# A two-part transformer at 256 positions in split float32: feed-forward products 512 columns wide, and the modulation rows summed on the vector engine

## The chip, the cores and the metric

The kernel runs on one core of one Trainium2 chip, as one program. The metric is device time in microseconds (us); lower is better. A core has a matrix engine (PE, with its weight loads shown as PEld), a vector engine (DVE), an activation engine (ACT), a general engine (POOL), a queue for transfers (SP) and 16 DMA engines. PE reads the on-chip memory SBUF and writes PSUM, which has eight banks of 2 KB for each of 128 partitions; a bank holds 512 float32 columns. Each engine works through its own instructions in order.

## The reference, cut to what matters

The input `x` has 256 positions of 1024 features. A first block does mixed attention, cross attention and a feed-forward. Two further layers follow, whose norms are shifted, scaled and gated by rows computed from a vector `c` ("modulation"). In each of them a gated feed-forward stands before and after a mixer.

```python
# first block
u = rms_norm(x, g_mlp[l]) @ w_up[l]                     # 1024 -> 4096
x = x + jnp.square(jax.nn.relu(u)) @ w_down[l]          # 4096 -> 1024
...
# second block, two layers
mod = c_act @ ada_w[l] + ada_b[l]                       # 1024 -> 9 * 1024
sh1, sc1, g1, sh2, sc2, g2, sh3, sc3, g3 = jnp.split(mod, N_ADA, axis=-1)
h = modulate(x, norm_g[l, 0], sh1, sc1)
x = x + 0.5 * g1[:, None] * swiglu(h, ff_w13[l, 0], ff_w2[l, 0])   # a, b = h @ w13; (silu(a) * b) @ w2
...                                                     # layer 0: convolution and attention; layer 1: sparse attention
h = modulate(x, norm_g[l, 2], sh3, sc3)
x = x + 0.5 * g3[:, None] * swiglu(h, ff_w13[l, 1], ff_w2[l, 1])
```

The inner width of `swiglu` is 2816, which is 22 blocks of 128. `c_act` is the SiLU of `c`.

## The kernel before

Everything is held transposed: features on the 128 partitions, the 256 positions (`S`) as columns. A weight matrix is cut into tiles of 128 x 128. To keep float32 accuracy with PE's faster 32-bit form (`fp32r`), each weight and each activation is split in two: a rounded `hi` and the rest `lo = value - hi`. A product is three matmuls, `hi*hi + hi*lo + lo*hi`, all added up in PSUM (`mm3`, line 358): weights `wh`, `wl` are PE's stationary operand, activations `xh`, `xl` its moving one, 256 columns each time. Every matmul loads its own weights.

Weights stream in units of 1 MB (`raw`, [128 x 2048], four buffers, issued on SP in `issue`, line 386). `pump` (line 402) splits half a unit at a time: ACT writes `whi` (line 329), DVE writes `wlo` (line 415), three half units ahead of use. A half unit feeds 8 weight tiles and is called a *step* here. The program is a list of steps in an order written out in Python, and every engine's order follows from it.

`pairs` (line 462) makes two blocks of 128 outputs at a time: 2 x 8 weight tiles, two steps, both results side by side in one PSUM bank. It serves `w_up` (16 pairs), `w13` (22 pairs, four times) and smaller products. The first 2 or 3 pairs of a `w13` (`head`) have a form of their own, with two more columns for the shift. `singles` (line 516) makes one block of 128 outputs at a time; without `early` it serves `w_down` (8 blocks of 32 tiles) and `w2` (8 blocks of 22 tiles, four times).

After a pair, `evac_up` (line 1353) or `evac` in `ff` (line 1403) takes the result out of PSUM (ReLU and square, or SiLU and product, on DVE and ACT), and the result is split into `gh` (ACT) and `gl` (DVE, line 353), deferred to the next step. After a single, `evac` in `residual` (line 1268) adds it to `x` (DVE, line 1271 or 1273), and `norm_part` starts the next norm from it.

The modulation rows are the second stream. `ada_steps` (line 714) needs 9 x 8 slices of [128 x 1024] for each of two layers, two slices to a unit of 1 MB that goes through the same four `raw` buffers. Each slice is times one number per partition and added up in `adacc`: for the first slice of a sum ACT writes `adacc`; for the other seven ACT scales the slice in place and POOL adds it (line 737), in halves of 512 columns. `with_ada` (line 783) spreads these pieces behind the steps from the first attention to the middle of the third `w2`. `rows` then lets PE add up `adacc` over the partitions, two steps after the last piece.

`self.g` gives [128 x 256] buffers from a ring of 64 (`GP`). The lines on which the counting of matmuls and of modulation pieces rests (361 and 736 to 737):

```python
prod = [(wh, xh), (wh, xl), (wl, xh)]
...
self.act(src, src, scale=scale)
nc.gpsimd.tensor_tensor(half, half, src, OP.add)
```

## Time and profile before

| | us |
|---|---|
| median of 3 runs | 1494.89 (1494.23 to 1496.46) |
| the profiled execution | 1491.65 |
| its span, first to last instruction | 1489.9 |
| PE busy in the span | 1437.3 |
| DVE busy | 1059.5 |
| ACT busy | 918.9 |
| POOL busy | 633.6 |

A line of a profile names line, engine, operation, the tiles written and read, shapes, count, busy time, the mean of one in ns, and what ended the engine's idle time before it. PE's matmuls overlap, so the time that one costs is the distance from its start to the next one's start, not its row's duration.

### The profile page before, as it was taken

Reading aid. Unit: us, or ns where it says so; the run is one execution under the profiler, and the core shown is the slowest. Engines: PE = TensorE matmul, PEld = TensorE weight load, DVE = VectorE, ACT = ScalarE, POOL = GpSimd, SP = SyncE. Lnnn points to the kernel's source line nnn. Section 1 sums busy time; section 2 is a strip of 40 time slices with the busy share of each in tenths; the row PEclk is TensorE's granted clock in tenths of the full one; section 3 lists DMA queues with packets and bytes.
Section 4 is the critical chain, followed back from the end, with each engine's and each line's share of the span. In section 5 each row is a group of like instructions: output and inputs, shape, how many; then the busy total and the mean of one; then the engine's idle time right before and its main releaser. Section 6 shows DMA issues by size and latency. Waiting matters only on the chain.

```text
span 1489.9 us, 28338 instructions
## 1 busy us (share of the span) xinstructions
PE 1437.3 (96%) x11478; PEld 1374.9 (92%) x11478; DVE 1059.5 (71%) x1643; ACT 918.9 (62%) x1666; POOL 633.6 (43%) x466
## 2 busy tenths in 40 slices
PE   8998999999999999998899999999999999999997
PEld 8886989999989989998799999999999887999997
DVE  7877767776658777689887776677765788765553
ACT  6546767777657567664667666676654665644442
POOL 3002433545874566753356658546453200500021
PEclk9999999999999999999999999999999999999998
DMA  8344646777665777754447877568773620355451
GB/s 319 116 142 170 218 151 227 244 270 273 260 246 199 278 267 272 257 186 170 169 171 272 295 262 296 206 238 300 259 278 132 219 80 25 118 198 196 173 182 45
DMA packets 46067, 312.00 MB, mean 209 GB/s; under 512 B 5232, under 2 KB 7024, under 8 KB 9072
## 3 DMA queue, kind: packets, MB, share of 16 engines
q1 hardware_dynamic: 45936, 310.19, 57.8%
q8 instruction: 90, 1.47, 0.4%
q14 instruction: 41, 0.34, 0.1%
HBM read 309.12 MB, written 1.05 MB: 208 GB/s over the span
## 4 chain that ended last, share of the span: by engine, by line
PE 64%; DVE 16%; ACT 8%; DMA 7%; issue 2%; POOL 1%; SPq 0%; POOLq 0%; ACTq 0%; DVEq 0%
PE mm L356 57%; DVE wlo L415 6%; DMA raw<-w 4%; ACT whi L329 2%; ACT raw L329 2%; PE sc L356 2%; PE o L356 1%; DVE p L849 1%; POOL adacc L737 1%; PE mmt L356 1%; DVE hlo L664 1%; DMA raw<-w_up 1%; DMA raw<-w_down 1%; DVE gl L353 1%; ACT p L329 1%
## 5 line engine op out<-in xcount | busy, mean ns | idle before, releaser
L415 DVE TENSOR_TENSOR wlo<-raw,whi 128x1024 fp32r<-128x1024 f32 (+2 forms) x438 | 627.2, 1438 | 52.2 <-ACT whi L329 51.7
L737 POOL TENSOR_TENSOR adacc<-adacc,raw 128x512 f32<-128x512 f32 x252 | 430.8, 1734 | 415.8 <-ACT raw L329 331.4
L356 PE MATMUL mm<-hlo,whi 128*128 128x256 f32 x1960 | 556.6, 284 | 6.0 <-DVE hlo L664 4.1
L356 PE MATMUL mm<-hhi,whi 128*128 128x256 f32 (+1 forms) x1960 | 558.0, 285 | 1.5 <-ACT whi L329 1.5
L356 PE MATMUL mm<-hhi,wlo 128*128 128x256 f32 (+1 forms) x1960 | 553.3, 282 | 5.2 <-DVE wlo L415 5.2
L329 ACT ACTIVATE whi<-raw 128x1024 fp32r<-128x1024 f32 (+2 forms) x438 | 453.2, 1044 | 110.6 <-DMA raw<-w 72.5
L356 PEld LDWEIGHTS mm<-hlo,whi 128*128 128x128 f32 x1960 | 369.9, 189 | 9.6 <-DVE hlo L664 5.6
L356 PEld LDWEIGHTS mm<-hhi,wlo 128*128 128x128 f32 x1960 | 371.2, 189 | 7.3 <-DVE wlo L415 7.0
L356 PEld LDWEIGHTS mm<-hhi,whi 128*128 128x128 f32 x1960 | 370.2, 189 | 5.4 <-DVE wlo L415 1.7
L356 PE MATMUL mm<-gh,whi 128*128 128x256 f32 x960 | 272.6, 284 | 0.0
L356 PE MATMUL mm<-gh,wlo 128*128 128x256 f32 x960 | 271.6, 283 | 0.0
L356 PE MATMUL mm<-gl,whi 128*128 128x256 f32 x960 | 271.6, 283 | 0.0
L356 PEld LDWEIGHTS mm<-gh,whi 128*128 128x128 f32 x960 | 184.2, 192 | 4.3 <-issue 3.4
L356 PEld LDWEIGHTS mm<-gl,whi 128*128 128x128 f32 x960 | 184.2, 192 | 0.0
L356 PEld LDWEIGHTS mm<-gh,wlo 128*128 128x128 f32 x960 | 184.2, 192 | 0.0
L329 ACT ACTIVATE raw<-raw,sc 128x512 f32<-128x512 f32 x252 | 167.0, 712 | 0.6 <-DMA raw<-ada 0.5
L1410 DVE TENSOR_TENSOR ft<-mm,ft 128x256 f32<-128x256 f32 x79 | 33.4, 423 | 110.0 <-ACT ft L329 109.8
L353 DVE TENSOR_TENSOR gl<-ft,gh 128x256 fp32r<-128x256 f32 x120 | 74.0, 628 | 46.2 <-ACT gh L329 46.0
L580 POOL TENSOR_SCALAR xg<-x,M 128x256 f32<-128x256 f32 x40 | 55.9, 1398 | 97.4 <-DVE x L1273 91.2
L329 ACT ACTIVATE p<-sc,nm 128x128 f32<-128x128 f32 (+1 forms) x120 | 49.8, 420 | 66.5 <-DVE r L840 18.7
L329 ACT ACTIVATE ft<-mm 128x256 f32<-128x256 f32 x79 | 29.9, 379 | 96.3 <-PE mm L356 96.1
L596 POOL TENSOR_TENSOR acc<-acc,sq 128x256 f32<-128x256 f32 x60 | 60.8, 1016 | 43.5 <-ACT sq L329 37.0
(298 smaller groups left out, 1878.6 us busy)
## 6 DMA issues: line engine op xcount, KB each, us to landing
raw<-w SPq DMA_DIRECT2D x132, 1024.0 KB, 4.9
raw<-ada SPq DMA_DIRECT2D x72, 1024.0 KB, 6.4
raw<-w_up SPq DMA_DIRECT2D x16, 1024.0 KB, 5.0
raw<-w_down SPq DMA_DIRECT2D x16, 1024.0 KB, 5.2
raw<-hy_in SPq DMA_DIRECT2D x8, 1024.0 KB, 5.2
raw<-w_in SPq DMA_DIRECT2D x6, 1024.0 KB, 7.8
raw<-nsa_in SPq DMA_DIRECT2D x6, 1024.0 KB, 5.0
raw<-w_ck SPq DMA_DIRECT2D x4, 1024.0 KB, 4.9
```

What stands on the lines that cost most here:

```text
L329: return self.nc.scalar.activation(out, in_, func, **k)
L353: self.nc.vector.tensor_tensor(lo, src, hi.bitcast(F), OP.subtract)
L356: self.nc.tensor.matmul(out, lhsT, rhs, start=start, stop=stop, skip_group_check=True)
L415: self.behind = lambda hi=hi[:, :b - a], lo=lo[:, :b - a], src=src: self.nc.vector.tensor_tensor(lo, src, hi.bitcast(F), OP.subtract)
L580: nc.gpsimd.tensor_scalar(st["xg", c], xc, gain(c), None, op0=OP.mult)
L596: nc.gpsimd.tensor_tensor(acc, st["acc" + key], sq, OP.add)
L664: nc.vector.scalar_tensor_tensor(*last, op0=OP.add, op1=OP.subtract)
L737: nc.gpsimd.tensor_tensor(half, half, src, OP.add)
L849: nc.vector.tensor_scalar(p[n], p[n], r[:, n:n + 1], None, op0=OP.mult)
L1410: nc.vector.tensor_mul(s, ps[:, 1, :], s)
```

## The change

Four things change.

1. Activations are held as one buffer with `lo` and `hi` side by side (`h`: [`lo` | `hi` | two shift columns] for each block; `gg` and others through `two`: [`hi` | `lo`]). For `w_up`, for the `w13` pairs behind the heads and for `w_down` and `w2`, a weight tile takes two matmuls and not three: `wh` against both halves, 512 columns, into a whole PSUM bank, and `wl` against the `hi` half, 256 columns, added to one half of that bank (`mm2`). The other products keep three.
2. The two halves of the bank are joined after the product: in `pairs` by `summed` (ACT copies one half, DVE adds the other), with the rest of `evac` deferred by one step and the split by two; in `residual` by a second addition to `x`. A wide pair uses two banks, one from tag `mm` and one from tag `T`; the banks of `ada` move from `T` to `O`.
3. A modulation slice is one instruction of 1024 columns: ACT for the first of a sum, DVE's scalar_tensor_tensor (times the number, plus `adacc`) for the other seven. ACT's scaling and POOL's additions are gone.
4. `self.g` gives halves of [128 x 2 x 256] buffers from a ring of 32.

```diff
+    def summed(self, pss):
+        ts = [self.t("ft") for _ in pss]
+        for t, ps in zip(ts, pss):
+            self.act(t, ps[:, 0, :])
+        for t, ps in zip(ts, pss):
+            self.nc.vector.tensor_add(t, ps[:, 1, :], t)
+        return ts
...
+    def mm2(self, out, w, x, start, stop):
+        (wh, wl), (xh, _, both) = w, x[:3]
+        self.mm(out.rearrange("p a b -> p (a b)"), wh, both, start=start, stop=False)
+        self.mm(out[:, self.hi_at(x), :], wl, xh, start=False, stop=stop)
...
     def flush(self):
-        for f in self.deferred:
+        now, self.deferred = self.deferred, []
+        for f in now:
             f()
-        self.deferred.clear()
...
-                        if r == 0:
+                        if r == 0 and wide:
+                            state["ps"] = [self.ps("mm", [P, 2, S], "mm"), self.ps("mm", [P, 2, S], "T")]
+                        elif r == 0:
                             state["ps"] = self.ps("mm", [P, 2, S], tags[pr % 2])
-                        self.mm3(state["ps"][:, m, :], w, (xh, xl), start=r == 0, stop=k == kc - 1)
+                        if wide:
+                            self.mm2(state["ps"][m], w, x(k), start=k == 0, stop=k == kc - 1)
+                        else:
+                            self.mm3w(state["ps"][:, m, :], w, (xh, xl), start=r == 0, stop=k == kc - 1)
...
             def fn(raw):
-                if k == 0 and b == 0:
+                if k == 0:
                     st["acc", s] = self.w("adacc", [P, D], bufs=2)
...
                 if k == 0:
-                    self.act(half, src, scale=scale)
+                    self.act(acc, src, scale=scale)
...
                 else:
-                    self.act(src, src, scale=scale)
-                    nc.gpsimd.tensor_tensor(half, half, src, OP.add)
+                    nc.vector.scalar_tensor_tensor(acc, src, scale, acc, op0=OP.mult, op1=OP.add)
...
-                if gate is None:
-                    nc.vector.tensor_add(xc, ps, xc)
-                else:
-                    nc.vector.scalar_tensor_tensor(xc, ps, gate(m), xc, op0=OP.mult, op1=OP.add)
+                for part in (ps,) if len(ps.shape) == 2 else (ps[:, 0, :], ps[:, 1, :]):
+                    if gate is None:
+                        nc.vector.tensor_add(xc, part, xc)
+                    else:
+                        nc.vector.scalar_tensor_tensor(xc, part, gate(m), xc, op0=OP.mult, op1=OP.add)
...
-                nc.vector.scalar_tensor_tensor(t, ps[:, m, :], 0.0, stu["rbs"], op0=OP.max, op1=OP.mult)
-                self.act(t, t, AF.Square)
...
+            for m, t in enumerate(self.summed(ps)):
+                g = gg[2 * pr + m] = self.two("gg")
+                def up(g=g, t=t):
+                    nc.vector.scalar_tensor_tensor(t, t, 0.0, stu["rbs"], op0=OP.max, op1=OP.mult)
+                    self.act(t, t, AF.Square)
+                    self.deferred.append(lambda: self.split(g[0], g[1], t))
+                self.deferred.append(up)
...
-                self.act(s, ps[:, 0, :], AF.Silu)
-                nc.vector.tensor_mul(s, ps[:, 1, :], s)
...
+            s, t = self.summed(ps)
+            def up():
+                self.act(s, s, AF.Silu)
+                nc.vector.tensor_mul(s, t, s)
+                self.deferred.append(lambda: self.split(g[0], g[1], s))
+            self.deferred.append(up)
```

PE at the border of two pairs in the second `w13`. `mm` is the PSUM bank, `hhi`, `hlo` and `h` are the activations, `whi` and `wlo` the weights. Before, the last tile of one pair and the first of the next:

```order
L356 MATMUL mm_10694<-hhi_9006,whi_10611 128x256
L356 MATMUL mm_10694<-hlo_9007,whi_10611 128x256
L356 MATMUL mm_10694<-hhi_9006,wlo_10612 128x256
L356 MATMUL mm_10764<-hhi_9006,whi_10647 128x256
L356 MATMUL mm_10764<-hlo_9007,whi_10647 128x256
L356 MATMUL mm_10764<-hhi_9006,wlo_10648 128x256
```

After, the last tile of one pair and the first two of the next:

```order
L385 MATMUL mm_8896<-h_7818,whi_8828 128x512
L385 MATMUL mm_8896<-h_7818,wlo_8829 128x256
L385 MATMUL mm_8951<-h_7818,whi_8855 128x512
L385 MATMUL mm_8951<-h_7818,wlo_8856 128x256
L385 MATMUL mm_8952<-h_7818,whi_8855 128x512
L385 MATMUL mm_8952<-h_7818,wlo_8856 128x256
```

A tile has two rows and not three, and the two results of a pair stand in two banks.

DVE in the same `w13`, a little over one pair. `ft` is the pair's result on its way, `gl` and `gg` the split result, `adacc` the modulation sum. Before:

```order
L1410 TENSOR_TENSOR ft_10675<-mm_10619,ft_10675 128x256
L415 TENSOR_TENSOR wlo_10648<-raw_10464,whi_10647 128x1024
L353 TENSOR_TENSOR gl_10679<-ft_10675,gh_10678 128x256
L415 TENSOR_TENSOR wlo_10687<-raw_10464,whi_10686 128x1024
L1410 TENSOR_TENSOR ft_10747<-mm_10694,ft_10747 128x256
L415 TENSOR_TENSOR wlo_10720<-raw_10615,whi_10719 128x1024
```

After:

```order
L377 TENSOR_TENSOR ft_8936<-mm_8895,ft_8936 128x256
L377 TENSOR_TENSOR ft_8937<-mm_8896,ft_8937 128x256
L785 SCALAR_TENSOR_TENSOR adacc_8739<-raw_8777,sc_683,adacc_8739 128x1024
L456 TENSOR_TENSOR wlo_8914<-raw_8832,whi_8913 128x1024
L1466 TENSOR_TENSOR ft_8936<-ft_8937,ft_8936 128x256
L785 SCALAR_TENSOR_TENSOR adacc_8739<-raw_8777,sc_683,adacc_8739 128x1024
L456 TENSOR_TENSOR wlo_8944<-raw_8832,whi_8943 128x1024
L382 TENSOR_TENSOR gg_8935<-ft_8936,gg_8935 128x256
```

Between two weight splits there now stand two joins, or a modulation slice, that were not on DVE; this pair has two slices, others have one or none.

ACT in the same place. `raw` scaled in place is the modulation slice. Before:

```order
L329 ACTIVATE whi_10719<-raw_10615 128x1024
L329 ACTIVATE ft_10747<-mm_10694 128x256
L329 ACTIVATE raw_10539<-raw_10539,sc_707 128x512 x2
L329 ACTIVATE whi_10756<-raw_10615 128x1024
L329 ACTIVATE gh_10750<-ft_10747 128x256
```

After:

```order
L349 ACTIVATE gg_8877<-ft_8878 128x256
L349 ACTIVATE ft_8936<-mm_8895 128x256
L349 ACTIVATE ft_8937<-mm_8896 128x256
L349 ACTIVATE whi_8943<-raw_8832 128x1024
L349 ACTIVATE ft_8936<-ft_8936 128x256
```

Two copies out of PSUM stand where the SiLU stood, the SiLU (`ft<-ft`) comes one weight split later, and the two scalings are gone.

## Rows read from the trace of the kernel before

**Rows 1.** The page: busy time of each engine, share of the span, instructions.

```profile
PE 1437.3 (96%) x11478; PEld 1374.9 (92%) x11478; DVE 1059.5 (71%) x1643; ACT 918.9 (62%) x1666; POOL 633.6 (43%) x466
```

**Rows 2.** The chain in order of time: start, length, what (us).

```profile
773.22 83.28 PE mm L356 x695
...
1304.67 167.41 PE mm L356 x1397
```

**Rows 3.** Stretches: length, then busy PE, PEld, DVE, ACT, POOL; clock, DMA share, GB/s.

```profile
265.00:343.00 78.00, 75.52 (x618) 73.14 (x617) 58.37 (x76) 59.40 (x106) 42.86 (x28) 1.00 0.74 261
...
643.00:756.00 113.00, 100.65 (x774) 92.50 (x773) 97.56 (x179) 67.88 (x142) 48.19 (x45) 0.98 0.48 171
...
776.00:887.00 111.00, 111.00 (x931) 110.03 (x930) 80.45 (x85) 78.23 (x124) 65.39 (x36) 1.00 0.76 273
...
1306.00:1416.00 110.00, 110.00 (x924) 110.00 (x923) 61.21 (x84) 50.84 (x79) 0.00 (x0) 1.00 0.55 192
```

**Rows 4.** The page's costliest groups.

```profile
L737 POOL TENSOR_TENSOR adacc<-adacc,raw 128x512 f32<-128x512 f32 x252 | 430.8, 1734 | 415.8 <-ACT raw L329 331.4
...
L329 ACT ACTIVATE whi<-raw 128x1024 fp32r<-128x1024 f32 (+2 forms) x438 | 453.2, 1044 | 110.6 <-DMA raw<-w 72.5
...
L356 PE MATMUL mm<-gh,whi 128*128 128x256 f32 x960 | 272.6, 284 | 0.0
...
L329 ACT ACTIVATE raw<-raw,sc 128x512 f32<-128x512 f32 x252 | 167.0, 712 | 0.6 <-DMA raw<-ada 0.5
...
L329 ACT ACTIVATE ft<-mm 128x256 f32<-128x256 f32 x79 | 29.9, 379 | 96.3 <-PE mm L356 96.1
```

**Rows 5.** PE in order of time, in the cross-attention values: start, duration, what (us).

```profile
133.88 0.39 PE L356 MATMUL mm<-wlo,hmh 128*128 128x512 f32 x1
...
135.04 0.39 PE L356 MATMUL mm<-whi,hmh 128*128 128x512 f32 x1
135.27 0.39 PE L356 MATMUL mm<-wlo,hmh 128*128 128x512 f32 x1
...
136.17 0.39 PE L356 MATMUL mm<-whi,hml 128*128 128x512 f32 x1
```

**Rows 6.** What PE waited for: total us, times, longest.

```profile
PE mm L356 <- DVE wlo L415: 5.2, 8, 1.9
...
PE ada L356 <- POOL adacc L737: 3.8, 4, 1.2
```

**Rows 7.** DVE in order of time in the second `w13` (us).

```profile
802.10 0.51 DVE L353 TENSOR_TENSOR gl<-ft,gh 128x256 fp32r<-128x256 f32 x1 [0.92 <-ACT gh L329]
802.53 2.31 DVE L415 TENSOR_TENSOR wlo<-raw,whi 128x1024 fp32r<-128x1024 f32 x1
805.36 0.42 DVE L1410 TENSOR_TENSOR ft<-mm,ft 128x256 f32<-128x256 f32 x1 [0.51 <-ACT ft L329]
...
811.11 0.42 DVE L1410 TENSOR_TENSOR ft<-mm,ft 128x256 f32<-128x256 f32 x1 [1.47 <-ACT ft L329]
811.45 1.22 DVE L415 TENSOR_TENSOR wlo<-raw,whi 128x1024 fp32r<-128x1024 f32 x1
```

**Rows 8.** DVE's groups in 776 to 887 us, the second `w13`.

```profile
L353 DVE TENSOR_TENSOR gl<-ft,gh 128x256 fp32r<-128x256 f32 x20 | 13.6, 678 | 10.1 <-ACT gh L329 10.1
L1410 DVE TENSOR_TENSOR ft<-mm,ft 128x256 f32<-128x256 f32 x19 | 8.0, 424 | 19.1 <-ACT ft L329 19.1
```

**Rows 9.** DVE's groups in 265 to 343 us, `w_up`.

```profile
L1356 DVE SCALAR_TENSOR_TENSOR ft<-mm,rbs 128x256 f32<-128x256 f32 x24 | 8.9, 412 | 1.0 <-PE mm L356 1.0
```

**Rows 10.** DVE's groups in 887 to 954 us, the second `w2`.

```profile
L1273 DVE SCALAR_TENSOR_TENSOR x<-mm,M,x 128x256 f32<-128x256 f32 x7 | 3.3, 477 | 1.9 <-PE mm L356 1.9
```

**Rows 11.** POOL's modulation additions by stretch: length, busy POOL (count), clock, DMA share, GB/s.

```profile
265.00:343.00 78.00, 42.86 (x28) 1.00 0.74 261
643.00:756.00 113.00, 20.92 (x16) 0.98 0.48 171
776.00:887.00 111.00, 65.39 (x36) 1.00 0.76 273
```

More of the change, by code (lines that the diff above doesn't have):

```diff
@@ L303, in __init__, with two @@
         self.flip, self.now = 0, None
+        self.half = {}
         self.deferred, self.behind = [], None
     def g(self, name, dt=F, shape=None):
-        return self.gp.tile(shape or [P, S], dt, name=name, tag="g")
+        key = (name if name in PAIRED else "", dt)
+        t = self.half.pop(key, None)
+        n = 1
+        if t is None:
+            n = 0
+            t = self.half[key] = self.gp.tile([P, 2, S], dt, name=name, tag="g")
+        ap = t[:, n, :]
+        if shape:
+            names = " ".join(f"d{i}" for i in range(len(shape) - 1))
+            ap = ap.rearrange(f"p ({names}) -> p {names}", **{f"d{i}": x for i, x in enumerate(shape[1:])})
+        return ap
+    def two(self, name):
+        if name == "gg":
+            self.half.clear()
+        t = self.gp.tile([P, 2, S], R, name=name, tag="g")
+        return t[:, 0, :], t[:, 1, :], t.rearrange("p a b -> p (a b)")
     def w(self, name, shape, dt=F, tag=None, bufs=2):
@@ L495, in fn @@
                     w = (hi[:, o:o + P], lo[:, o:o + P])
[L496 to L497 removed]
+                    xh, xl = x(k)[:2]
                     if pr < head:
@@ L703, in dst, with h_part @@
             if c == 0:
[L704 to L708 removed]
+                self.h = self.work.tile([P, KD, 2 * S + 2], R, name="h", tag="h", bufs=1)
+            return self.h_part(c)
+        return dst
+    def h_part(self, c):
+        return self.h[:, c, S:2 * S], self.h[:, c, :S], self.h[:, c, :2 * S], None
     def h_src(self):
[L711 removed]
+        return self.h_part
     def ada_steps(self, l):
@@ L776, in ada_steps @@
             for q in range(4):
-                steps.append([piece(s, q, n) for n in range(4)])
+                steps.append([piece(s, q, n) for n in range(2)])
             if s % 2 or s == 8:
@@ L899, in split_out @@
     def split_out(self, ps, name, scale=None):
-        hi, lo = self.g(name + "h", R), self.g(name + "l", R)
+        pair = self.two(name)
+        hi, lo = pair[:2]
         if scale is None:
@@ L905, in split_out @@
             self.nc.vector.scalar_tensor_tensor(lo, ps, scale, hi.bitcast(F), op0=OP.mult, op1=OP.subtract)
-        return hi, lo
+        return pair
     def zeroed(self, name, keep):
@@ L965, in late_loads @@
         nc.sync.dma_start(self.posi[1], self.dram["pos"][:, 1, :])
-        self.mem = [self.g(f"mem{c}") for c in range(KD)]
+        self.mem = [self.g("mem") for c in range(KD)]
         for c in range(KD):
@@ L1067, in mdst @@
         def mdst(c):
-            hm[c] = (self.g(f"hmh{c}", R), self.g(f"hml{c}", R))
+            hm[c] = self.two("hm")
             return hm[c]
@@ L1353, in evac_up @@
         def evac_up(pr, ps):
-            for m in range(2):
-                t = self.t("ft")
-                nc.vector.scalar_tensor_tensor(t, ps[:, m, :], 0.0, stu["rbs"], op0=OP.max, op1=OP.mult)
-                self.act(t, t, AF.Square)
-                gh, gl = self.g("gh", R), self.g("gl", R)
-                self.deferred.append(lambda gh=gh, gl=gl, t=t: self.split(gh, gl, t))
-                gg[2 * pr + m] = (gh, gl)
-        gsrc = (lambda k: gg[k][0], lambda k: gg[k][1])
+            for m, t in enumerate(self.summed(ps)):
[5 more added lines that the diff above has]
+                self.deferred.append(up)
+        gsrc = lambda k: gg[k]
         self.gg, self.gsrc = gg, gsrc
-        mlp = self.pairs("w_up", h, KD, evac_up, npairs=16, st=stu)
+        mlp = self.pairs("w_up", h, KD, evac_up, npairs=16, st=stu, wide=True)
         M = self.M[0]
@@ L1460, in evac_z @@
                         nc.vector.tensor_mul(a, src, a)
-                        hi, lo = self.g("yh", R), self.g("yl", R)
-                        self.split(hi, lo, a)
-                        y[c] = (hi, lo)
+                        y[c] = self.two("y")
+                        self.split(y[c][0], y[c][1], a)
         scale = 96 ** -0.5
```

99 lines of the change are left out of this document (48 added, 51 removed).

## The prediction

> **What bounds the kernel now.** I read the page's busy times first: PE 96% of the span, DVE 71%, ACT 62%, POOL 43% [rows 1]. A busy PE can still be waiting between matmuls, so the second view is the chain in order of time: in the second `w13` it is PE alone for 83.28 us and 695 matmuls, and in the last feed-forward for 167.41 us and 1397 [rows 2]. That is 0.1198 us from start to start both times: PE runs without a hole. The third view, stretches, says where this holds. In the second `w13` PE is busy for all of 111.0 us beside a DVE of 80.5, ACT of 78.2 and POOL of 65.4; in the last `w13`, which has no modulation work, for all of 110.0 [rows 3]. In `w_up` 75.5 of 78 are left, and in the mixer of layer 0 100.7 of 113, with DVE at 97.6 [rows 3]. The granted clock is 1.00 in the feed-forwards, the upper level of 2.4 GHz. So the feed-forwards, two thirds of the span, are bound by the time of a matmul; there an instruction taken from PE counts in full if weights and PSUM come free as fast. In the mixers the small waits between engines decide, and PE gains nothing there.
>
> **Matmuls, the main term.** The wide tiles are: `w_up` 16 pairs x 16 = 256, `w13` (4 x 22 - 9 head pairs) x 16 = 1264, `w_down` 8 x 32 = 256, `w2` 4 x 8 x 22 = 704; together 2480. (The last two are the 960 `gh` matmuls of each kind [rows 4].) A tile now costs 3 x 0.1198 = 0.3595 us. After, it is one matmul of 512 columns and one of 256. The cross-attention values have 512-column matmuls of the same kind, each with its own weights: 133.88 to 136.17 us is ten distances, 0.229 each [rows 5]. No row has 512 followed by 256 into half the bank, so the sum 0.229 + 0.1198 = 0.3488 is an estimate; it saves 0.0107 us a tile, **26.5 us** in all. Bounds: the five distances from 133.88 to 135.04 give 0.232, the four from 135.27 to 136.17 give 0.225 [rows 5]; with these a tile saves 0.0077 or 0.0147 us, 19.1 or 36.5 us in all. I take the mean of the ten, as `wh` and `wl` follow each other here as there.
>
> The Trainium skill (TensorE: Matmul & The Clock Gate, Back-to-back issue gap) gives columns / 2.4 GHz plus 2.5 ns per matmul at the full clock, 109 ns for 256 columns and 216 for 512; by that a merge would save 2.5 ns a tile, 6.2 us in all. The trace differs, with 119.8 and 229, so by its rows the part of a matmul that does not grow with its columns is about 10.7 ns. A rival below is built on this doubt.
>
> **Modulation, off POOL and ACT.** POOL loses all 252 additions, 430.8 us, and ACT 252 scalings of 0.71 us [rows 4]. DVE gains 126 instructions of 1024 columns. Before has none; a weight split of that size takes 1.22 us when POOL is quiet [rows 7], and a number per partition adds 0.05 (0.477 against 0.424 on 256 columns [rows 8, 10]), so 1.27; four 256-column ones, 1.91, are the upper bound, 1.22 the lower. In a row of DVE instructions the next starts 0.08 us before the row of the last ends (811.11 plus 0.42 against 811.45 [rows 7]), so each costs the queue 0.08 less: 1.19. In return DVE is no longer slowed: the split takes 2.31 beside POOL and 1.22 without [rows 7].
>
> **Does DVE keep up?** Per pair of a `w13`: two splits of 1.14, two joins, one product and one `lo` of 0.34, together 3.64 us. The second `w13` has 36 half additions in 111 us [rows 11], so 18 slices over some 19.3 pairs, 0.93 x 1.19 = 1.10. Sum 4.74 against 16 x 0.3488 = 5.58 of PE. With 1.91 it is 5.3, still below. So the added DVE work is hidden under PE; without that cover 18 slices and 39 joins would be 35 us here alone. In `w_up` a pair has two ReLUs (0.33 each, from PSUM [rows 9]) and two `lo`: 4.30, plus 14 slices over 13 pairs [rows 11], 1.28, makes 5.58 against 5.58: a tie. With 1.91 it is 6.27, 9 us over the 13 pairs. I take 2 us for a tie that is not always hit, 0 to 9 as bounds. Behind a waiting slice on DVE stand the next weight split and the joins; the split due next is needed two steps, 5.6 us, after the pair's end and would be done 3.6 after it (a copy of 0.38, two joins, a slice, the split), so some 2 us of a delay are hidden.
>
> ACT in the second `w13` loses 36 x 0.71 = 25.6 of 78.2 us and gains about 20 copies of 0.38 [rows 3, 4, 11]. It is nowhere near the bound. The joins also stand between a pair and its split, but the value is first read in `w2` after 21 tiles, 7 us later: nothing. The ring of 32 double buffers holds as much as the 64; I cost it at nothing, since what is paired is made and read together.
>
> **Waits.** PE waited 3.8 us in four places for POOL's last addition before `rows` [rows 6]. DVE has two whole steps for it, about 5.6 us: **-3.8**. The 5.2 us for `wlo` [rows 6] I leave as they are; POOL's absence shortens them, DVE's new work lengthens them. The second addition to `x` is behind the last matmul of the whole kernel: 0.477 less the overlap, **+0.4**. At the four inner ends of a feed-forward the same 0.4 stands before a norm that PE reaches only after a further step: 0, at most 2. In the mixer of layer 0 16 half additions, 8 slices, fall on a DVE that is busy 97.6 of 113 [rows 3, 11]: if all lie on the path +9.5; the 20.9 us of POOL that now leave DVE alone give back up to half, -10, and ACT loses 16 x 0.71. I take 0, and 5 either way for all mixers. SP's order of transfers is unchanged; a modulation unit's buffer is given back by DVE and not by POOL.
>
> **Sum** on the profiled execution: 1491.65 - 26.5 + 2 - 3.8 + 0.4 = 1463.8. It was 3.2 us below the median of the runs, so I forecast 1467 us.
>
> **Rival 1: the weight stream does not go faster.** Four `raw` buffers carry both streams. DMA is busy 0.76 in the second `w13` against 0.55 in the last [rows 3], and ACT's `whi` waited 72.5 us for weights in all [rows 4]. If the ring is at its limit wherever both streams run, only the other tiles gain: three pairs of `w_up`, the last `w13` and `w2`, 48 + 320 + 176 = 544 x 0.0107 = 5.8 us, and 1494.9 - 5.8 + 0.4 = 1489.5. Against it: PE shows no hole there [rows 2], ACT waits with three half units in hand, and the wish is for 3% more on 0.76. Chance 0.10.
>
> **Rival 2: a merge saves nothing.** If the 0.229 of 512 columns owes something to that stretch and a matmul's time goes with its columns alone, 512 take 2 x 0.1198, and only the waits are won: 1494.9 - 3.8 + 0.4 = 1491.5. Against it: the ten distances, with a spread of 3%, lie below 0.2396 [rows 5]. Chance 0.05. The Trainium skill's 2.5 ns a matmul, named above, lies between this and the forecast, at 1494.9 - 6.2 - 3.4 = 1485; the same ten distances speak against it, and it has no more than a part of the 0.05.
>
> **Rival 3, slower: DVE waits in its own order.** In the second `w13` DVE stood idle 10.1 us before 20 `gl`, waiting for ACT, and 19.1 before 19 products [rows 8], 1.5 us per pair. Some of that is only DVE being early: the 1.47 and 0.51 before the product wait for PE's pair by way of ACT, but the 0.92 before `gl` is ACT's order [rows 7]. The joins and the deferred product add links DVE-ACT-DVE. If 1.5 us a pair stay, a `w13` pair with slices takes 6.24 and a `w_up` pair 7.08, against 5.75 and 6.0 (78 us / 13) before: 59 x 0.49 + 13 x 1.08 = +43 us, less 14.2 on the other 1328 tiles and 3.8: 1494.9 + 25 = 1520. It decides from 1.15 us a pair on. Against it: a weight split stands between each pair of links, 1.14 us in which ACT can answer, and ACT's scalings, which held `gh` back, are gone. Chance 0.07.
>
> **How the numbers follow.** Forecast 0.72, rival 1 0.10, rival 2 0.05, rival 3 0.07, and 0.06 for more than forecast (mixers freed of POOL, the fast bound of a tile), below 1455. The range goes from 1455 (the fast bound of a tile: 1494.9 - 36.5 - 3.8 + 0.4) up to rival 1 at 1489.5, and so takes in the slow tile together with 9 us in `w_up` (1482); it leaves out 0.18. Faster by over 0.2% (3 us, about what a measurement of this kernel can tell from no change): 0.72 + 0.10 + 0.06 + part of rival 2 = 0.90; within: 0.03; slower: 0.07.
>
> **What would show it.** PE's chain in the second `w13` at 0.349 us for two matmuls, its 20 wide pairs ending some 3.4 us earlier; POOL's `adacc` rows gone and `wlo` at 1.22 everywhere in `w13`; DVE at 85% there and near full in `w_up`; no wait of PE for `adacc`. Wrong, if 512 followed by 256 takes 0.36 (rival 2), if PE waits for `wlo` behind a DMA (rival 1) or for `wlo` and joins with DVE idle before ACT (rival 3).

## The result and the profile after

The changed kernel takes **1458.78 us** (median of 4 runs, 1455.91 to 1460.99) against 1495.2 of the kernel before beside it (4 runs, 1494.23 to 1496.46): ratio **0.9755, 95% interval 0.9735 to 0.9775**. The forecast was 1467 in a range of 1455 to 1489.5. The profiled execution took 1455.91 us, with a span of 1453.8; that of before had 1489.9.

First the page's busy times (busy us, share of the span, instructions), which answer [rows 1], and pieces of the chain in order of time (start, length, what), which answer [rows 2]:

```profile
PE 1410.9 (97%) x8998; PEld 1243.0 (85%) x8998; DVE 1156.2 (80%) x1999; ACT 821.8 (57%) x1586; POOL 212.0 (15%) x214
```

```profile
584.11 39.38 PE mm L385 x227
...
751.93 81.71 PE mm L385 x464
...
1271.98 163.22 PE mm L385 x932
```

The chain through these feed-forwards is still PE alone, with two matmuls to a tile and not three: 81.71 us for 464 is 0.352 us a tile in the second `w13`; 39.38 for 227 is 0.347 in a `w2`. Before, three made 0.3595. The same stretches as [rows 3], in the same columns (`w_up`, mixer of layer 0, second and last `w13`):

```profile
262.00:337.00 75.00, 73.58 (x416) 63.10 (x418) 70.19 (x113) 47.96 (x98) 0.00 (x0) 1.00 0.73 272
...
623.00:735.00 112.00, 102.04 (x780) 94.27 (x779) 95.11 (x188) 59.53 (x127) 27.33 (x30) 0.97 0.46 166
755.00:863.00 108.00, 108.00 (x620) 93.76 (x619) 93.68 (x139) 67.40 (x122) 0.00 (x0) 1.00 0.76 282
1274.00:1381.00 107.00, 107.00 (x612) 93.69 (x611) 73.43 (x122) 63.30 (x117) 0.00 (x0) 1.00 0.55 194
```

POOL's column is empty in the feed-forward stretches, DVE's has risen from 80.45 of 111 to 93.68 of 108 in the second `w13` and from 58.37 of 78 to 70.19 of 75 in `w_up`, and PE is busy in all or nearly all of each feed-forward stretch. Next the page's groups (instructions, busy us, mean ns, idle before and who ended it), to be read beside [rows 4]:

```profile
L456 DVE TENSOR_TENSOR wlo<-raw,whi 128x1024 fp32r<-128x1024 f32 (+2 forms) x438 | 539.2, 1236 | 11.3 <-ACT whi L349 10.6
...
L349 ACT ACTIVATE whi<-raw 128x1024 fp32r<-128x1024 f32 (+2 forms) x438 | 452.0, 1046 | 119.3 <-DMA raw<-w 80.8
L785 DVE SCALAR_TENSOR_TENSOR adacc<-raw,sc,adacc 128x1024 f32<-128x1024 f32 x126 | 164.0, 1301 | 0.2 <-ACT adacc L349 0.2
L377 DVE TENSOR_TENSOR ft<-mm,ft 128x256 f32<-128x256 f32 x190 | 72.1, 419 | 48.9 <-ACT ft L349 48.8
```

The 126 slices are on DVE at 1.30 us; the 252 rows of POOL are gone, and `wlo` has a mean of 1.236 us. The joins are the 190 rows of the helper's line 377. What PE's matmuls waited for (us in all, times, longest), against [rows 6]:

```profile
PE sc L385 <- ACT p L349: 6.1, 6, 2.6
PE mm L385 <- DVE h L714: 4.4, 7, 1.1
PE mm L385 <- DVE q L1557: 3.5, 1, 3.5
PE mm L385 <- DVE wlo L456: 3.5, 6, 1.0
```

No row of `adacc` is left. A stage ledger shows where the 36 us lie. It goes from each stage's first matmul to the next one's, in us; the middle column is the first experiment below, where the modulation alone is moved.

| stage | before | modulation moved | changed |
|---|---|---|---|
| start to `w_up` | 243.1 | 241.3 | 241.2 |
| `w_up` | 100.2 | 95.7 | 96.5 |
| `w_down` | 97.5 | 94.3 | 92.8 |
| `w13`, `w2` | 136.6, 65.1 | 131.4, 65.1 | 129.7, 62.8 |
| mixer of layer 0 | 113.6 | 111.8 | 111.8 |
| `w13`, `w2` | 130.5, 67.7 | 130.5, 65.0 | 128.4, 62.8 |
| `w13`, `w2` | 130.6, 65.5 | 130.6, 65.1 | 128.4, 63.6 |
| mixer of layer 1 | 137.2 | 136.4 | 136.8 |
| `w13`, `w2` and end | 128.9, 73.4 | 128.9, 73.6 | 126.8, 72.2 |

### The profile page after: what moved, and what is told of

The parts are those of the page before. It is cut to its first block, busy times and chain, and to the rows that moved or that the text cites. A ratio compares the mean times of both kernels' runs of the same rounds, so it can differ in the third digit from the quotient of the medians.

```text
span 1453.8 us, 23211 instructions
## 1 busy us (share of the span) xinstructions
PE 1410.9 (97%) x8998; PEld 1243.0 (85%) x8998; DVE 1156.2 (80%) x1999; ACT 821.8 (57%) x1586; POOL 212.0 (15%) x214
## 3 DMA queue, kind: packets, MB, share of 16 engines
q8 instruction: 70, 1.15, 0.3%
## 4 chain that ended last, share of the span: by engine, by line
PE 76%; DVE 16%; ACT 4%; DMA 2%; issue 2%; POOL 0%; SPq 0%; POOLq 0%; ACTq 0%; DVEq 0%
PE mm L385 68%; DVE wlo L456 4%; DVE adacc L785 2%; PE sc L385 2%; PE o L385 2%; PE mmt L385 1%; DVE h L714 1%; ACT p L349 1%; DVE gg L382 1%; DMA raw<-w_in 1%; ACT whi L349 1%; PE ada L385 1%; PE pT L904 1%; DVE p L897 1%; PE ssum L385 1%
## 5 line engine op out<-in xcount | busy, mean ns | idle before, releaser
L385 PE MATMUL mm<-h,whi 128*128 128x512 f32 (+2 forms) x2400 | 710.1, 358 | 6.3 <-DVE h L714 4.4
L385 PE MATMUL mm<-h,wlo 128*128 128x256 f32 (+1 forms) x1960 | 553.6, 282 | 3.5 <-DVE wlo L456 3.5
L456 DVE TENSOR_TENSOR wlo<-raw,whi 128x1024 fp32r<-128x1024 f32 (+2 forms) x438 | 539.2, 1236 | 11.3 <-ACT whi L349 10.6
L349 ACT ACTIVATE whi<-raw 128x1024 fp32r<-128x1024 f32 (+2 forms) x438 | 452.0, 1046 | 119.3 <-DMA raw<-w 80.8
L385 PEld LDWEIGHTS mm<-h,whi 128*128 128x128 f32 x2400 | 425.9, 190 | 80.9 <-DVE h L714 8.2
L385 PEld LDWEIGHTS mm<-h,wlo 128*128 128x128 f32 x1960 | 371.3, 189 | 6.3 <-DVE wlo L456 5.9
L385 PE MATMUL mm<-gg,whi 128*128 128x512 f32 x960 | 337.1, 397 | 0.0
L385 PE MATMUL mm<-gg,wlo 128*128 128x256 f32 x960 | 267.5, 279 | 0.0
L385 PEld LDWEIGHTS mm<-gg,whi 128*128 128x128 f32 x960 | 180.2, 188 | 46.9 <-issue 4.2
L385 PEld LDWEIGHTS mm<-gg,wlo 128*128 128x128 f32 x960 | 180.7, 188 | 0.1
L785 DVE SCALAR_TENSOR_TENSOR adacc<-raw,sc,adacc 128x1024 f32<-128x1024 f32 x126 | 164.0, 1301 | 0.2 <-ACT adacc L349 0.2
L349 ACT ACTIVATE ft<-mm 128x256 f32<-128x256 f32 x190 | 65.5, 377 | 73.1 <-PE mm L385 72.9
```

Of the source, the lines that this page charges most:

```text
L349: return self.nc.scalar.activation(out, in_, func, **k)
L385: self.nc.tensor.matmul(out, lhsT, rhs, start=start, stop=stop, skip_group_check=True)
L456: self.behind = lambda hi=hi[:, :b - a], lo=lo[:, :b - a], src=src: self.nc.vector.tensor_tensor(lo, src, hi.bitcast(F), OP.subtract)
L785: nc.vector.scalar_tensor_tensor(acc, src, scale, acc, op0=OP.mult, op1=OP.add)
```

## Experiments

Two theories divide the 36 us that were won. **A**: some 22 come from the merged matmuls, between the prediction's slow bound of 19.1 and its 26.5, and some 14 from moving the modulation off POOL and ACT. **B**: the move wins the 4 us of the prediction, and the merge some 32. The first runs left a third question: why the move is worth so much. Every ratio below is to the kernel before, run beside that experiment; its own median lay between 1491.9 and 1495.9 us.

**e1_ada_dve: the modulation alone.** The kernel before, with this:

```diff
-ADA_LAGS = (0, 0, 1, 1, 3, 4)
+ADA_LAGS = (0, 1, 3, 4)
...
-                    self.act(src, src, scale=scale)
-                    nc.gpsimd.tensor_tensor(half, half, src, OP.add)
+                    nc.vector.scalar_tensor_tensor(acc, src, scale, acc, op0=OP.mult, op1=OP.add)
```

> The kernel before, with the modulation slices as 126 scalar_tensor_tensors of 1024 columns on DVE and nothing else of the change: three matmuls per tile, buffers and joins as before. Theory A (the change won some 22 us from merged matmuls and some 14 us from taking the modulation off POOL and ACT): 1495 - 14 = 1481 us, with the time won at the places where PE waited for POOL's last addition and for wlo. Theory B (nearly all of the 36 us is from the matmuls, the modulation is worth the 3.8 us that PE waited for POOL): 1491 us.

Measured: 1472.74 us, ratio 0.9866 (0.9843 to 0.9889), span 1469.7: 20 us, more than either theory gave. The view the prediction left out is what PE's weight loads waited for, here of the kernel before (us in all, times, longest):

```profile
PEld ada L356 <- POOL adacc L737: 9.7, 9, 2.1
PEld mm L356 <- DVE wlo L415: 8.6, 11, 2.1
```

A matmul's weights are loaded ahead of it, and where the stationary operand is the late one (`adacc` is that of `rows`) the wait stands in the load's row. From the matmul before `rows` to the one after it, four of the ten groups took 3.01 to 4.36 us in the kernel before; in this run all take 1.19 to 1.21. The sum over the ten is 10.9 us, not the 3.8 of the matmuls' own rows [rows 6]. The ledger's first `w_up`, `w_down`, `w13` and the second `w2` hold them. The rest, some 9 us, lies in the same stages, in the start and in the mixer; PE's waits for `wlo` fall from 5.2 us to 1.8 in the matmuls' view.

Where the rest may come from, the chain shows. Here is a piece of it in `w_up` of the kernel before (start, length, what):

```profile
286.43 2.32 DVE wlo L415
288.75 0.02 SPq L394
...
288.80 4.83 DMA raw<-w_up
...
293.72 1.06 ACT whi L329
294.78 0.61 ACT ft L329 x2
295.39 1.23 ACT raw L329 x2
```

A split of 2.32 us gives its buffer back late, SP issues the next weights only then, they take 4.83 us, and ACT's copy of them has two scalings behind it. In the kernel before such transfers of weights are 16.7% of the chain in `w_up`, 15.5% in `w_down` and 22.8% in the first `w13`; in this run they are on the chain in none of the three, and 96% of the chain through `w_up` is PE's matmuls.

**e3_three: everything but the merge.** The changed kernel with three matmuls of 256 columns in `mm2`, joins kept:

```diff
-        self.mm(out.rearrange("p a b -> p (a b)"), wh, both, start=start, stop=False)
-        self.mm(out[:, self.hi_at(x), :], wl, xh, start=False, stop=stop)
+        n = self.hi_at(x)
+        self.mm(out[:, n, :], wh, xh, start=start, stop=False)
+        self.mm(out[:, 1 - n, :], wh, x[1], start=False, stop=False)
+        self.mm(out[:, n, :], wl, xh, start=False, stop=stop)
```

> The changed kernel with three matmuls of 256 columns per tile into the two halves of the bank, so joins, buffers and modulation on DVE stay and only the merge is undone. Theory A: a tile takes 0.359 us and not 0.350 again, 2480 tiles, +22 us: 1481 us, the same as the modulation alone. Theory B: +32 us, 1491. If the joins cost something on the way, this run lies above the modulation alone by that.

Measured: 1475.56 us, ratio 0.9886 (0.9863 to 0.991), span 1472.5. So the joins, with the deferral, the buffers and the banks that come with them, cost 2.8 us over e1 by the spans (by the ratios 0.002, within the intervals), and the merge is worth 1472.5 - 1453.8 = **18.7 us** (by the ratios 0.0131, 19.6 us). By the ledger's stages it gives 1.8 to 3.1 us in each `w13`, 1.3 to 2.3 in each `w2`, 1.5 in `w_down` and 0.3 in `w_up`. A missed the time by 5 us and B by 15, since they put the move at 14 and at 4; B falls.

**e2_wide: the merge without the move.** The changed kernel with the modulation on ACT and POOL as before:

> The changed kernel with the modulation slices back on ACT (scaling) and POOL (addition, halves of 512 columns): two matmuls per tile and the joins stay. Theory A: 1495 - 22 = 1473 us, or a few us more, since DVE then has the joins and is slowed by POOL as well (a w13 pair: 3.64 plus 2 x 0.5 of slower splits, 4.7, below PE's 5.6). Theory B: 1495 - 32 = 1463 us.

Measured: **1518.09 us, ratio 1.0169 (1.0138 to 1.0201)**: slower than the kernel before, which no theory had. PE's waits, and the second `w13` in the columns of [rows 3]:

```profile
PE mm L386 <- DVE wlo L457: 21.0, 33, 1.7
PE ada L386 <- POOL adacc L790: 9.9, 9, 1.9
```

```profile
790.00:908.00 118.00, 113.96 (x635) 96.00 (x635) 101.56 (x130) 87.78 (x160) 60.62 (x35) 1.00 0.70 260
```

PE has holes in `w13`, which it had in neither parent. Its wait at the ten groups of `rows` comes to 22.8 us here, 10.9 in the kernel before, and its weight loads waited 35.0 us for `wlo`, 8.6 before. So the two halves of the change are not additive. The joins and shorter tiles ask more of DVE in less time; that POOL slows this DVE and ACT's scalings keep it waiting is what the next runs were to take apart.

**e4_double: how much room has DVE?** The changed kernel, behind each slice a second one whose result nobody uses:

```diff
+                    nc.vector.scalar_tensor_tensor(src, src, scale, acc, op0=OP.mult, op1=OP.add)
```

> The changed kernel with a second scalar_tensor_tensor of 1024 columns on DVE behind each modulation slice, into the slice itself: its result is not used, so the outputs are the same. It doubles DVE's modulation work, +126 x 1.2 us. By the prediction's budget a w13 pair then needs 4.74 + 1.10 = 5.84 us of DVE against 5.62 of PE, a w_up pair 6.86 against 5.62: 59 x 0.2 + 13 x 1.2 = +28 us, 1487 us, with PE waiting for wlo in w_up above all. If DVE waited in its own order already (rival 3), more than +60 us. If DVE had more room than the budget says, less than +8 us.

Measured: 1560.97 us, ratio 1.0455 (1.043 to 1.048), span 1558.8, that is 105 us for 126 more instructions of 1.3 us, 164 us of DVE. The expected 1487 us was missed by 74. The cover that the prediction spoke of is thin: PE waits for the splits behind them.

```profile
PE mm L385 <- DVE wlo L456: 56.2, 62, 1.9
```

Two other things moved, so the 105 us are not DVE's alone. The added instruction writes the raw buffer and so holds it: 14.36 us from landing to reuse on the mean (200 to 1250 us), 11.05 in the changed kernel, and `whi` waited 99.3 us for weights, 80.8 there. And the mean granted clock was 0.985 against 0.994. As the lower level, 1.2 GHz, is half the upper, an estimate from these two and the spans is 2 x (0.015 x 1558.8 - 0.006 x 1453.8) = 29 us more at the lower level, which costs at most half of that, 15 of the 105 us. By its expectation, more than 60 us meant that DVE waits in its own order already; with these in it the run does not decide that.

**e6_act_dve: ACT's scalings back, POOL idle.** The changed kernel, with ACT scaling each slice and DVE adding it:

```diff
-                    nc.vector.scalar_tensor_tensor(acc, src, scale, acc, op0=OP.mult, op1=OP.add)
+                    self.act(src, src, scale=scale)
+                    nc.vector.tensor_tensor(acc, acc, src, OP.add)
```

> The changed kernel, but ACT scales each 1024-column slice in place and DVE adds it (one tensor_tensor), so ACT's scalings are back and POOL stays free. It takes apart why the wide tiles with the modulation on ACT and POOL ran at 1518 us. Theory C: ACT's scalings, standing ahead of the weight copies and of the joins' copies in ACT's order, made that kernel slow; then this one is slow too, 1500 us or more, with DVE idle behind ACT before joins and products. Theory D: POOL's additions, which slow DVE's two-input instructions, made it slow; then this one is at 1458 to 1466 us, with wlo at about 1.24 us.

Measured: 1497.69 us, ratio 1.0033 (1.002 to 1.0046), some 40 us behind the changed kernel and 2 short of theory C's 1500, with theory D out, although DVE's additions are shorter than the fused slices (1.223 against 1.301 us) and `wlo` is at 1.228. What DVE waited for, one row; then DVE and PE in `w_up` in order of time (start, length, what, idle before):

```profile
DVE adacc L786 <- ACT raw L349: 85.8, 77, 3.4
```

```profile
298.50 0.75 DVE L1409 SCALAR_TENSOR_TENSOR ft<-ft,rbs 128x256 f32<-128x256 f32 x2
300.77 1.23 DVE L786 TENSOR_TENSOR adacc<-adacc,raw 128x1024 f32<-128x1024 f32 x1 [1.53 <-ACT raw L349]
301.92 1.22 DVE L456 TENSOR_TENSOR wlo<-raw,whi 128x1024 fp32r<-128x1024 f32 x1
303.19 0.39 PE L385 MATMUL mm<-h,wlo 128*128 128x256 f32 x1 [1.52 <-DVE wlo L456]
```

DVE stands in its own order for ACT's scaling, the next weight split stands behind it, and PE waits for the split: the mechanism of rival 3, in a place the prediction had not named. By the ledger's stages e6 loses 13.2 us ahead of `w_up`, 10.8 in `w_up`, 7.3 in the mixer of layer 0, 4.4 and 5.5 in the first two `w2` and 2.8 in `w_down` and the first `w13`; in the second and third `w13` nothing. In `w_up` one transfer of weights is on the chain, of 4.74 us, as in the changed kernel (4.77), so there it is DVE's wait for ACT. Over the whole run transfers are 7% of the chain against 2%, and a modulation buffer was held 12.40 us against 11.05; so elsewhere late buffers may have a part, which no run separates. The granted clock, 0.988 against 0.994, is at most 9 us by the estimate made for e4. In the kernel before it was POOL that stood waiting for ACT, 331.4 us [rows 4], with fewer engines behind it.

**e7_wide_pool and e8_narrow_pool: POOL's additions without ACT's scalings**, once with wide tiles (e2_wide) and once in the kernel before:

```diff
-                    self.act(src, src, scale=scale)
                     nc.gpsimd.tensor_tensor(half, half, src, OP.add)
```

> The wide tiles with the modulation on POOL, as in the run of 1518 us, but without ACT's scalings: POOL adds the slices as they come, which leaves the factor of the modulation out of what is computed. So POOL's additions are there and ACT's scalings are not. Theory C (ACT's order): 1458 to 1470 us. Theory D (POOL beside DVE): 1500 us or more, with wlo at 1.4 us on the mean and PE waiting for wlo and for the last addition. If it lies between, each has its part.

> The kernel before with the same one edit: ACT's scalings left out (and with them the factor of the modulation), POOL adds the slices as they come. It takes apart the 20 us that moving the modulation to DVE alone was worth. Theory C (ACT's scalings): most of the 20 us comes here too, about 1475 us. Theory D (POOL: the wait for its last addition and the slower DVE beside it): nearly nothing comes, 1488 to 1493 us, with PE's waits for the last addition still there.

Measured: e7 1508.87 us, ratio 1.0107 (1.0086 to 1.0129); e8 1502.93, ratio 1.0067 (1.0047 to 1.0088). With ACT's work gone, e8 should have been no slower than before, by either theory. Something else had moved, which the groups of `whi` show (e7, then e8):

```profile
L350 ACT ACTIVATE whi<-raw 128x1024 fp32r<-128x1024 f32 (+2 forms) x438 | 452.4, 1046 | 176.1 <-DMA raw<-w 114.1
```

```profile
L329 ACT ACTIVATE whi<-raw 128x1024 fp32r<-128x1024 f32 (+2 forms) x438 | 452.2, 1045 | 234.4 <-DMA raw<-w 156.3
```

Before it was 72.5 [rows 4]: the weights come later. SP waited up to 15.2 us for POOL to give a modulation buffer back, 8.8 in the kernel before, and the weight units stand behind it in SP's order. A modulation buffer was not held longer for that: 10.31 us from landing to reuse on the mean in e8, 12.23 in the kernel before. So neither run isolates what it was meant to, and why the weights come later is not settled. They led to the next three.

**e10_pool_load: POOL beside DVE, nothing else.** The changed kernel, with this beside each slice:

```diff
+                    for _ in range(5):
+                        nc.gpsimd.tensor_tensor(self.w("idle", [P, 192], bufs=1), self.colp[:, :192],
+                                                self.colp[:, 192:384], OP.add)
...
-        colp = self.c("colp", [P, COLP.size])
+        colp = self.colp = self.c("colp", [P, COLP.size])
```

> The changed kernel; beside each of the 126 modulation slices POOL makes five additions of 192 columns of a constant into a scratch tile that nobody reads (about 430 us of POOL in all, as its 252 additions took in the kernel before). No raw buffer waits for them, nor does PE or ACT; POOL's own later work stands behind them. Theory S (POOL slows DVE, whose splits and lo products take up to twice as long beside it): wlo at 1.4 us on the mean, PE waiting for wlo, 1485 us or more. Theory R (the raw ring): 1458 to 1465 us although DVE's rows are longer.

Measured: **1579.33 us, ratio 1.056 (1.0542 to 1.0577)**, 120 us more than the changed kernel, from work on which no split, no slice and no raw buffer waits. POOL was loaded more than meant (622 us instead of 430), so the size is not that of the kernel before; the mechanism is plain in the groups of the page (POOL) and of DVE, shapes apart:

```profile
L787 POOL TENSOR_TENSOR idle<-colp 128x192 f32<-128x192 f32 x630 | 622.1, 987 | 47.2
```

```profile
L456 DVE TENSOR_TENSOR wlo<-raw,whi 128x1024 fp32r<-128x1024 f32 x431 | 601.9, 1402 | 8.8 <-ACT whi L349 8.4
L785 DVE SCALAR_TENSOR_TENSOR adacc<-raw,sc,adacc 128x1024 f32<-128x1024 f32 x126 | 186.3, 1479 | 0.2 <-ACT adacc L349 0.2
L382 DVE TENSOR_TENSOR gg<-ft,gg 128x256 fp32r<-128x256 f32 x120 | 76.0, 644 | 8.5 <-ACT gg L349 8.2
L377 DVE TENSOR_TENSOR ft<-mm,ft 128x256 f32<-128x256 f32 x190 | 71.4, 414 | 37.8 <-ACT ft L349 37.8
```

```profile
PE mm L385 <- DVE wlo L456: 54.3, 53, 3.0
```

Three of these forms have grown: splits, slices (1301 to 1479 ns on the mean) and `lo` products (to 644). The join, of the same 256 columns, has not (419 and 414): one of its operands is in PSUM, while the others read both from SBUF. PE waits 54.3 us for splits, against 3.5. The weights are no rival here: `whi` waited 69.3 us for them, less than the 80.8 of the changed kernel. Two other parts are in the 120 us: of POOL's own later work PE waited for the norms' sums, 16.8 us; and the mean granted clock was 0.976 against 0.994, which by the estimate made for e4 is at most 29 us.

The Trainium skill (SBUF — State Buffer, "SBUF: two separate sides") says that VectorE and GpSimd share a port pair as an exclusive lock, and that an instruction with two SBUF inputs takes it against a GpSimd instruction that reads SBUF. The groups above agree: rows with two SBUF operands grew, the row with one in PSUM did not.

**e9_hold, e12_hold3: how tight is the ring of raw buffers?** The changed kernel, with a copy of one column of a modulation buffer after its second slice: in e9 on POOL, one step later, in e12, shown here, on DVE, two steps later:

```diff
-ADA_LAGS = (0, 1, 3, 4)
+ADA_LAGS = (0, 1, 3, 3, 4)
...
+                if n == 2:
+                    nc.vector.tensor_copy(self.w("held", [P, 1], bufs=2), raw[:, 2047:2048])
+                    return
...
-            return Step(fn, (f"ada{l}", 4 * s + q), raw=True, more=n < 1)
+            return Step(fn, (f"ada{l}", 4 * s + q), raw=True, more=n < 2)
...
-                steps.append([piece(s, q, n) for n in range(2)])
+                steps.append([piece(s, q, n) for n in range(3)])
```

> The changed kernel; behind each modulation unit, one step after its second slice, POOL copies one column of the unit's buffer (0.1 us of POOL, nothing on DVE, ACT or PE), so that only the time for which the buffer is held grows, by about one step of 2.8 us. In the kernel before, a modulation buffer in w_down was held 11.0 us from its landing to its reuse, in the changed kernel 8.9. Theory R (the ring of four raw buffers is what POOL's additions and ACT's scalings cost): the weight stream falls behind as in the kernel before, whi waits more for DMA, and the time goes up by 5 us or more, to 1464 or above. Theory S (the port that POOL shares with DVE, or the order on the engines): within 2 us of the changed kernel, 1457 to 1461.

> The copy of one column once more, now on DVE and two steps behind a unit's second slice, because POOL's copy in the earlier run went through as soon as the buffer had landed and held it hardly longer (11.5 us from landing to reuse on the mean against 11.05). DVE's order now puts the release some 5 us later at the price of 72 copies of one column, some 5 us of DVE in all. Theory R (the raw ring): modulation buffers held 14 us or more, whi waits longer for DMA, and the time rises by 10 us or more, to 1469 or above. Theory S (POOL beside DVE, and ACT's order): no more than the 72 copies, 1459 to 1464 us, whatever whi waits.

Measured: e9 1460.84 us, ratio 0.9767 (0.9746 to 0.9788), no difference; but POOL's copy ran when the data landed and the mean hold grew by 0.45 us only, so it tells nothing. e12 took **1474.23 us, ratio 0.9871 (0.9849 to 0.9893)**: 17 us more than the changed kernel by the ratios. A modulation buffer was held 12.38 us from landing to reuse on the mean (200 to 1250 us), 11.05 in the changed kernel, less than meant. Two groups of e12:

```profile
L349 ACT ACTIVATE whi<-raw 128x1024 fp32r<-128x1024 f32 (+2 forms) x438 | 452.9, 1047 | 198.2 <-DMA raw<-w 143.8
```

```profile
L778 DVE COPY held<-raw 128x1 f32<-128x1 f32 x72 | 10.6, 147 | 0.0
```

The copies took 10.6 us of DVE, not 5; even if all of that lay on the path, 6 us are left, and `whi` waits 143.8 us for weights against 80.8. So the ring is close to its limit. In e1 that wait is no different (72.2 against 72.5 in the kernel before), but a buffer was held 11.09 us there and 12.23 in the kernel before, and the chain under e1 has late weights in the stages that the move shortened. So the ring stays a possible part of what the move won.

**e11_lag0: both slices behind one step**, so that a buffer comes free earlier (`ADA_LAGS = (0, 0, 3, 4)`):

> The changed kernel with both slices of a modulation unit put behind the same step, so that its buffer comes free about one step, 2.8 us, earlier, at the price of two slices of 1.28 us in a row on DVE. Theory R (the raw ring still holds the weight stream back): up to 5 us less, 1454 to 1457. Theory S (DVE's order): no gain, or a loss of some us from wlo standing behind 2.5 us of slices.

Measured: 1464.04 us, ratio 0.9789 (0.9769 to 0.9809). `whi` waits only 53.9 us for weights, yet the time is some 5 us longer (the two intervals just overlap): PE waits 7.0 us for `wlo`, twice as much. So the earlier buffer gives nothing that two slices in a row in front of a split do not take back.

**e5_row64: where a block of `h` starts.** The changed kernel, with a row of `h` of 528 columns instead of 514:

```diff
-                        xs = self.h[:, k, S:]
+                        xs = self.h[:, k, S:2 * S + 2]
...
-                self.h = self.work.tile([P, KD, 2 * S + 2], R, name="h", tag="h", bufs=1)
+                self.h = self.work.tile([P, KD, 2 * S + 16], R, name="h", tag="h", bufs=1)
```

> The changed kernel, only the row of h, which the w13 matmuls read, widened from 514 to 528 columns, so that each of its 8 blocks starts on a multiple of 64 bytes as in the w2 source. In the changed kernel a tile took 0.3515 us in w13 and 0.349 in w2. Theory A: the odd start of the blocks costs the difference; the 1520 tiles of w_up and w13 win 0.0025 us each, 3.8 us in all, ratio about 0.973 to the kernel before. Theory B: the difference comes from how weights and buffers arrive; the time stays that of the changed kernel, ratio 0.9755 within 0.001.

Measured: 1458.17 us, ratio 0.9771 (0.9747 to 0.9796): no gain. In the last `w13` the 256-column distance goes from 0.1187 to 0.1171 us on the mean and the 512-column one from 0.2324 to 0.233, 1 ns a tile in all. No run beat the changed kernel by what these measurements can tell.

## Why the prediction was right, and where its steps were off

The sign, the bound and the order of events held; the time came out 8 us below the forecast and 3.8 above the range's lower end. By the spans 1489.9 - 20.2 (move) + 2.8 (joins) - 18.7 (merge) gives the 1453.8 of the changed kernel, by construction. The prediction's sum had -3.8, +2.4 and -26.5 for these. Two terms were mis-sized in opposite directions, the merge too large by 7.8 us and the move too small by 16.4, so the near hit is part luck.

**The merge** was put at 26.5 us and measured 18.7 (19.6 by the ratios), at the slow bound of 19.1. Of [rows 5] I took the mean of ten distances, 0.229. In the changed kernel PE in order of time, in the second `w13`, reads (start, length, what):

```profile
800.12 0.40 PE L385 MATMUL mm<-h,whi 128*128 128x512 f32 x1
800.36 0.28 PE L385 MATMUL mm<-h,wlo 128*128 128x256 f32 x1
800.48 0.39 PE L385 MATMUL mm<-h,whi 128*128 128x512 f32 x1
800.71 0.28 PE L385 MATMUL mm<-h,wlo 128*128 128x256 f32 x1
800.83 0.39 PE L385 MATMUL mm<-h,whi 128*128 128x512 f32 x1
```

That is 0.35 to 0.36 from one tile's start to the next. Over that stretch the means are 0.2331 after a 512-column matmul and 0.1189 after a 256-column one, 0.352 a tile; in `w2` 0.2333 and 0.1160, 0.349. The five distances of 0.232 in [rows 5] were the nearest. The reason given for the mean of the ten does not hold either: in those rows `whi` and `wlo` are the moving operand and `hmh`, `hml` the stationary one, the other way round than here. Rival 2 is out, as 18.7 us is not nothing. The Trainium skill's fixed 2.5 ns a matmul (TensorE: Matmul & The Clock Gate, Back-to-back issue gap), which that section gives for a matmul by itself and not for a stream of weight loads and matmuls, made an estimate of 6.2 us of this; the measured 18.7 are three times that.

**PE's wait for POOL** was put at 3.8 us, from the matmuls' own rows [rows 6]. Moving the modulation was worth 20.2: 10.9 are the whole wait at `rows`, most of which stands in the weight loads' rows. The rest is what POOL and ACT cost through DVE and the raw buffers, which I had costed at nothing for PE because PE showed no hole in the second `w13` [rows 2, 3]. It showed none there, and the second and third `w13` won nothing by the move. But the chain of `w_up` and of the first `w13` had lengthened splits, late weights and ACT's scalings on it (under e1), and I had not read it there. The gain is in the start, `w_up`, `w_down`, the first `w13`, a `w2` and the mixer.

**The joins and the tie in `w_up`** were put at +2 (0 to 9), the tail at +0.4; together they measured +2.8. A slice was put at 1.27 us, and the median is 1.276. DVE's share in the second `w13` was put at 85%, and is 93.68 of 108, 87%; in `w_up` it is 94%, with PE at 73.58 of 75. The estimate of 4.74 us a pair in the second `w13` stands too: 93.68 over 19.3 pairs is 4.85. The tie in `w_up` took what the merge gave: the stage has 96.5 us, 95.7 with the modulation moved alone, and its chain runs through DVE, with PE's matmuls 24% of it.

**Rival 1**, the weight stream, did not happen: DMA's share is the same 0.76 and `whi` waited 80.8 us for weights, 72.5 before, with no hole in PE's chain. But e12 shows how near it was.

**Rival 3**, DVE waiting in its order, did not happen in `w13`. DVE's groups there (755 to 863 us) against [rows 8]:

```profile
L377 DVE TENSOR_TENSOR ft<-mm,ft 128x256 f32<-128x256 f32 x38 | 14.3, 418 | 3.2 <-ACT ft L349 3.1
L382 DVE TENSOR_TENSOR gg<-ft,gg 128x256 fp32r<-128x256 f32 x19 | 8.0, 421 | 8.1 <-ACT gg L349 8.1
L1466 DVE TENSOR_TENSOR ft<-ft 128x256 f32<-128x256 f32 x19 | 7.9, 418 | 1.5 <-ACT ft L349 1.5
```

12.8 us of idle time over 19 pairs is 0.67 a pair, 1.5 before, and under the 1.15 from which the rival decides. Of the prediction's two reasons, that a split fills each gap and that ACT's scalings are gone, e6 does not bear out the second for this stage: with the scalings back the second `w13` takes 128.4 us as in the changed kernel. They do their harm where DVE is fuller or other work stands behind, as in `w_up`. So the rival had a mechanism that exists, in the wrong stage.

**What would show it:** 0.349 us for two matmuls was 0.352; the 20 wide pairs of the second `w13` that were to end 3.4 us earlier ended 2.1 earlier; `adacc` is gone from POOL and from PE's waits; `wlo` is at 1.216 in the second `w13` (47.4 us for 39), as said.

**Open:** how the 9 us that are left of the move divide between splits that POOL lengthens, ACT's scalings and late weights in the kernel before, all three of which are on its chain (e7 and e8 were to tell and did not), and the same for the 26 us by which e2 is slower than before. That each of the three can slow the wide kernel is shown by e10, e6 and e12.

## To carry to other kernels

Before costing a wait from the matmuls' rows, read the weight loads' rows too: a late stationary operand waits there. Read the chain in each stage and not in one: the stage with PE alone on it told nothing of the others. Work taken off POOL can be worth more than the waits for its results when DVE runs two-SBUF-operand instructions on the path (e10). Work given to DVE is cheap only while DVE has room (e4) and where it needs no other engine's answer, since everything behind it in DVE's order waits as well (e6). Two edits that seem independent can need each other: here the merge with its joins alone loses 1.7%, the move alone wins 1.3%, and both win 2.5%.

## What the runs showed of the hardware

DVE instructions with both operands in SBUF are lengthened when a POOL addition is under way as they begin, and those with one in PSUM are not. In order of time in e10, while POOL runs 192-column additions without a gap:

```profile
859.23 0.82 DVE L382 TENSOR_TENSOR gg<-ft,gg 128x256 fp32r<-128x256 f32 x1
859.85 6.70 POOL L787 TENSOR_TENSOR idle<-colp 128x192 f32<-128x192 f32 x6
859.97 0.74 DVE L377 TENSOR_TENSOR ft<-mm,ft 128x256 f32<-128x256 f32 x2
860.64 1.63 DVE L785 SCALAR_TENSOR_TENSOR adacc<-raw,sc,adacc 128x1024 f32<-128x1024 f32 x1
862.19 1.62 DVE L456 TENSOR_TENSOR wlo<-raw,whi 128x1024 fp32r<-128x1024 f32 x1
```

Each of the former is some 0.4 us longer than alone (0.82 against 0.42, 1.62 against 1.22), whatever its own length, and two joins take the usual 0.74. Beside POOL's 512-column additions the split grew by up to 1.1 us, to 2.31 [rows 7]: in these two cases the price goes with the length of POOL's instruction and not with DVE's.

Which of the two begins first decides. In the kernel before, 96 of the 103 splits that began during a 512-column addition took longer, 2.30 us in the median; of the 49 inside which one began none did, 1.22 on the mean. The two splits of [rows 7], at 802.53 and 811.45, are one of each, so the second is not a split beside a quiet POOL, as the prediction read it; its 1.22 us is right all the same, the mean of the 198 splits without POOL:

```profile
800.33 7.89 POOL L737 TENSOR_TENSOR adacc<-adacc,raw 128x512 f32<-128x512 f32 x4 [2.31 <-issue]
811.82 1.99 POOL L737 TENSOR_TENSOR adacc<-adacc,raw 128x512 f32<-128x512 f32 x1 [3.60 <-ACT raw L329]
```

A 256-column matmul behind a 512-column one starts the next after 0.116 to 0.119 us, less than the 0.1198 in a row of its own kind, and a 512-column one after 0.232 to 0.236.
